# Score products of a differential attention head: from two packed 128-row products per map to three 64-row products on the two halves of the array

## The chip, the cores and the metric

The kernel runs on one core of one Trainium2 chip. The metric is the device time of one execution in microseconds (us), the median of several runs. The profile shown is one execution that the hardware profiler recorded.

## The reference, cut to what matters

One layer of a hybrid encoder block on 512 tokens plus 16 meta tokens (L = 528 keys), 1024 channels, float32. After an RMSNorm, one projection gives the operands of two attention branches of eight heads each: stick-breaking attention, and differential attention. Then come gates, an output projection and a SwiGLU feed-forward. The change is in the differential branch:

```
dq = df_q.reshape(B, L_pad, DF_HEADS, 2, DF_HEAD_DIM)   # two maps of 64 channels each per head
dk = df_k.reshape(B, L_pad, DF_HEADS, 2, DF_HEAD_DIM)
s = jnp.einsum('bhcqd,bhckd->bhcqk', q, k) * (DF_HEAD_DIM ** -0.5)
s = jnp.where(mask, s - slope * dist, -jnp.inf)
p = jax.nn.softmax(s, axis=-1)
w = p[:, :, 0] - lam * p[:, :, 1]
o = jnp.einsum('bhqk,bhkd->bhqd', w, v)
```

So each head has two score maps (c = 0 and 1), and each map is a product over 64 channels. The channels of both maps together are the 128 columns that one projection block of a head gives.

## The kernel before, in words

All float32 products are made of parts: an operand is split into a high part (rounded to the format fp32r) and a low part (the rest), and a product is the sum of high by high, high by low and low by high (`mm3`, lines 159 to 161, three instructions on TensorE that add up in the same PSUM bank). Each TensorE product is a weight load (LDWEIGHTS, 128 columns of the stationary operand) and a matmul that streams the moving operand.

The attention part is a loop over 16 heads, eight of the stick-breaking branch (`sb_head`) and then eight of the differential branch (`df_head`). While a head's attention runs, TensorE also makes the projections of the next head: `sb_units` and `df_units` give a list of units (two for q, two for k, two for v), `y_units` gives the branch's output projection of earlier heads, and the loop at line 748 puts units between the stages of a head wherever the head yields. So the TensorE work of a head's attention stands in several short groups between long runs of projection products. Outside the opening part of the kernel, which is ordered by hand, a scheduler places the instructions by priorities; evacuations of PSUM are issued with `tc.high_priority`.

Projection q and k of a stick-breaking head are kept as four tiles on 128 partitions: `qh`, `ql` (high and low part) and `kh`, `kl`. For a differential head the layout differs: for each map c one tile `dq` holds the 64 rows of that map's high part on the map's own half of the partitions and the low part on the other half, and one tile `dk` holds the high and the low part of k, both twice, once on each half of the partitions. So `q_evac` and `k_evac` of `df_units` work on 64 partitions at a time (lines 419, 420, 426, 427), and once per map a DMA on the GpSimd queue copies 64 rows to the other half (line 429).

With this layout the scores of one map over one block of keys need two products, each on all 128 rows:

```
nc.tensor.matmul(o, lhsT=q[c][:, qs], rhs=k[c][:, 0, k0:k1], start=True, stop=False)
nc.tensor.matmul(o, lhsT=q[c][:, qs], rhs=k[c][:, 1, k0:k1], start=False, stop=True)
```

The first gives high by high plus low by high, the second high by low plus low by low (lines 446 and 447).

A head has four query blocks t of 128 rows. `scores(0)`, `scores(1)` and `scores(2)` cover 256, 272 and 400 columns of keys for both maps; `scores3(c)` covers two halves of 264 columns for one map. Score tiles `z` are two PSUM banks each, and there are two of them. VectorE adds the position bias and takes the row maximum (`biased`, line 450), ScalarE takes the exponential (line 474), VectorE normalises and combines the two maps (lines 477 to 480), and TensorE transposes the result (line 315, and line 327 for small leftover blocks, which use 64 or 32 rows). Another partial product is the transposition of 33 rows of parameters at line 715.

Of the kernel before, what the change touches and what calls it, by code (L numbers as in the profile page):

```python
# [9 lines left out]
F32 = mybir.dt.float32  # L10
F32R = mybir.dt.float32r
# [5 lines left out]
P = 128  # L17
# [22 lines left out]
def block_kernel(ctx: ExitStack, tc: tile.TileContext, x, meta, norm_mix_g, w_in, w_gate, b_gate,  # L40
# [239 lines left out]
    def v_units(key, d):  # L280
        vT = ap_.tile([P, L], F32, tag="vT", bufs=1, name="vT")

        def turn():

            vf = ap_.tile([P, 2, P], F32, tag="vf", bufs=2, name="vf")
            vh = ap_.tile([P, 3, P], F32R, tag="vh", bufs=2, name="vh")
            vl = ap_.tile([P, 3, P], F32R, tag="vl", bufs=2, name="vl")
            pt, p5 = tr_tile(), tr_tile()
            for j in range(4):
                nc.tensor.transpose(pt[:, j * P:(j + 1) * P], vT[:, j * P:(j + 1) * P], ident)  # L290
            pv = pt.rearrange("p (j c) -> p j c", c=P)
            nc.scalar.copy(vh, pv[:, 0:3])
            nc.vector.tensor_tensor(vl, pv[:, 0:3], vh.bitcast(F32), op=ALU.subtract)
            nc.scalar.copy(vf[:, 0], pt[:, 3 * P:4 * P])
            for t in range(NQ):
                nc.gpsimd.tensor_copy(v_s[:, 32 * t:32 * t + NM], vT[:, (t + 1) * P:(t + 1) * P + NM])  # L296
            nc.tensor.transpose(p5[:, 0:P], v_s, ident)
            nc.scalar.copy(vf[:, 1], p5[:, 0:P])
            d["v"] = (vf, vh, vl)

        return kv_units(key, lambda ps, s: nc.scalar.copy(vT[:, s], ps)), turn  # L301
# [41 lines left out]
        return lambda: turn((0, 1)), turn_rest, weighted  # L343


    def sb_units(h):
        d = {}
        qh = ap_.tile([P, SEQ], F32R, tag="qh", bufs=2, name="qh")
        ql = ap_.tile([P, SEQ], F32R, tag="ql", bufs=2, name="ql")
        kh = ap_.tile([P, L], F32R, tag="kh", bufs=2, name="kh")  # L350
        kl = ap_.tile([P, L], F32R, tag="kl", bufs=2, name="kl")
        d["q"], d["k"] = (qh, ql), (kh, kl)

        def q_evac(ps):
            nc.scalar.activation(qh, ps, AF.Copy, scale=SB_SCALE)
            nc.vector.scalar_tensor_tensor(ql, ps, SB_SCALE, qh.bitcast(F32), op0=ALU.mult, op1=ALU.subtract)

        def k_evac(ps, s):
            nc.scalar.copy(kh[:, s], ps)
            nc.vector.tensor_tensor(kl[:, s], ps, kh[:, s].bitcast(F32), op=ALU.subtract)  # L360

        vu, turn = v_units(("sb", h, 2), d)
        return d, halves(("sb", h, 0), xT, QT, q_evac, h == 0) + kv_units(("sb", h, 1), k_evac) + vu, turn

    def sb_head(h, d, o_h, o_l):
        qh, ql = d["q"]
# [39 lines left out]
        nc.vector.tensor_tensor(o_l, ps, o_h.bitcast(F32), op=ALU.subtract)  # L406


    def df_units(h):
        d = {}  # L410
        hs = (slice(0, 64), slice(64, 128))
        q = [ap_.tile([P, SEQ], F32R, tag=("qh", "ql")[c], bufs=2, name=f"dq{c}") for c in range(2)]
        k = [ap_.tile([P, 2, L], F32R, tag=("kh", "kl")[c], bufs=2, name=f"dk{c}") for c in range(2)]
        d["q"], d["k"] = q, k

        def q_evac(ps):
            for c in range(2):
                a, b = hs[c], hs[1 - c]
                nc.scalar.activation(q[c][a], ps[a], AF.Copy, scale=DF_SCALE)
                nc.vector.scalar_tensor_tensor(q[c][b], ps[a], DF_SCALE, q[c][a].bitcast(F32),  # L420
                                               op0=ALU.mult, op1=ALU.subtract)

        def k_evac(ps, s):
            for c in range(2):
                a = hs[c]
                nc.scalar.copy(k[c][a, 0, s], ps[a])
                nc.vector.tensor_tensor(k[c][a, 1, s], ps[a], k[c][a, 0, s].bitcast(F32), op=ALU.subtract)  # L427
                if s.stop == L:
                    nc.gpsimd.dma_start(k[c][hs[1 - c]].bitcast(F32), k[c][a].bitcast(F32))

        vu, turn = v_units(("df", h, 2), d)
        return d, halves(("df", h, 0), xT, QT, q_evac) + kv_units(("df", h, 1), k_evac) + vu, turn

    late = []

    def df_head(h, d, o_h, o_l):
        q, k = d["q"], d["k"]
        bias = ap_.tile([P, L], F32, tag="bias", name="bias")
        nc.gpsimd.tensor_scalar(bias, dist, -(2.0 ** -(h + 1)), None, op0=ALU.mult)
        mx = small.tile([P, NQ, 2], F32, tag="mx", name="mx", bufs=2)  # L440
        ls = small.tile([P, NQ, 2], F32, tag="ls", name="ls", bufs=2)
        prs = [ap_.tile([P, 2, 144 + t * P], F32, tag=f"w{t}", name="pr") for t in range(NQ)]

        def score(o, t, c, k0, k1):
            qs = slice(t * P, (t + 1) * P)
            nc.tensor.matmul(o, lhsT=q[c][:, qs], rhs=k[c][:, 0, k0:k1], start=True, stop=False)  # L446
            nc.tensor.matmul(o, lhsT=q[c][:, qs], rhs=k[c][:, 1, k0:k1], start=False, stop=True)  # L447

        def biased(t, c, zz, po, bb):
            nc.vector.tensor_tensor_reduce(po, zz, bb, scale=1.0, scalar=-3.0e38, op0=ALU.add, op1=ALU.max,  # L450
                                           accum_out=mx[:, t, c:c + 1])

        def scores(t):
            n = 144 + t * P
            z = z_tile()
            for c in range(2):
                score(z[:, c, 0:max(n, 256)], t, c, 0, max(n, 256))
            for c in range(2):
                biased(t, c, z[:, c, 0:n], prs[t][:, c], bias[:, L - n:L])
            maps(t)  # L460

        def scores3(c):
            two = lambda v: v.rearrange("p (a b) -> p a b", a=2)
            z = z_tile()
            for hf in range(2):
                score(z[:, hf, 0:HL], 3, c, hf * HL, (hf + 1) * HL)
            biased(3, c, z[:, :, 0:HL], two(prs[3][:, c]), two(bias))

        def maps(t):
            pr = prs[t]  # L470
            nm = small.tile([P, 2], F32, tag="nm", name="nm")
            nc.vector.tensor_scalar(nm, mx[:, t], -1.0, None, op0=ALU.mult)  # L472
            for c in range(2):
                nc.scalar.activation(pr[:, c], pr[:, c], AF.Exp, bias=nm[:, c:c + 1], accum_out=ls[:, t, c:c + 1])  # L474
            with tc.high_priority(offset=EVAC):
                rc = small.tile([P, 2], F32, tag="rc", name="rc")
                nc.vector.reciprocal(rc, ls[:, t])
                nc.vector.tensor_tensor(rc[:, 1:2], rc[:, 1:2], nlam, op=ALU.mult)
                nc.vector.tensor_scalar(pr[:, 0], pr[:, 0], rc[:, 0:1], csc, op0=ALU.mult, op1=ALU.mult)
                nc.vector.scalar_tensor_tensor(pr[:, 0], pr[:, 1], rc[:, 1:2], pr[:, 0], op0=ALU.mult, op1=ALU.add)  # L480

        scores(0)
        scores(1)
        yield 1
        if late:
            late.pop(0)()
        scores(2)
        yield 1
        scores3(0)
        yield 1  # L490
        scores3(1)
        maps(3)
        t1, t2, av = attn_out(lambda t, k0, k1: prs[t][:, 0, k0:k1], d, 64)
        yield 3 if h < NH - 1 else 2
        t1()
        yield 1
        t2()
        yield 1
        ps = av()
        of = ap_.tile([P, SEQ], F32, tag="of", name="of")  # L500
        sq = ap_.tile([P, SEQ], F32, tag="sq", name="sq")
        sqh = ap_.tile([P, SEQ], F32R, tag="a_h", name="sqh")
        sql = ap_.tile([P, SEQ], F32R, tag="a_l", name="sql")
        nc.scalar.copy(of, ps)
        eng = nc.gpsimd if h < NH - 1 else nc.vector
        eng.tensor_tensor(sq, of, of, op=ALU.mult)
        split(sqh, sql, sq, lo_eng=eng)

        def norm():
            pv = tr_tile()  # L510
            nc.tensor.matmul(pv, lhsT=ones_r, rhs=sql, start=True, stop=False)
            nc.tensor.matmul(pv, lhsT=ones_r, rhs=sqh, start=False, stop=True)
            nc.scalar.activation(sq, pv, AF.Ln, bias=eps_c)
            nc.scalar.activation(sq, sq, AF.Exp, scale=-0.5)
            nc.vector.scalar_tensor_tensor(sq, pv, var_max, sq, op0=ALU.is_le, op1=ALU.mult)
            nc.vector.tensor_tensor(of, of, sq, op=ALU.mult)
            nc.scalar.activation(o_h, of, AF.Copy, scale=g_sub)
            nc.vector.scalar_tensor_tensor(o_l, of, g_sub, o_h.bitcast(F32), op0=ALU.mult, op1=ALU.subtract)  # L518

        late.append(norm)  # L520
# [594 lines left out]
```

## Time and profile before

| what | value |
|---|---|
| median of 3 runs | 992.69 us (992.54 to 994.67) |
| the profiled execution's own time | 992.9 us |
| its span, first to last instruction | 991.1 us |
| mean granted TensorE clock | 0.995 of full speed |
| busy time of TensorE matmuls (PE) | 970.6 us, 6285 instructions |
| busy time of weight loads (PEld) | 877.1 us |
| VectorE (DVE), ScalarE (ACT), GpSimd (POOL) | 662.0, 534.0, 110.0 us |

PE and PEld are two rows of the same engine: a weight load can run while the matmul before it streams. Matmuls are pipelined and the end of each is modelled, so a row's duration is longer than what the instruction costs in a stream; the time that one costs is read from the distance between the starts of neighbouring rows. L446 is line 446 of the kernel. A form such as 128x264 names partitions and elements per partition; in the form 33*128 of a matmul the first number is the rows of the stationary operand and the second its columns.

### The profile page before, as it was taken

The page shows a single profiled execution, that of the slowest core. Times are in us where ns is not written, and L with a number is a line of the kernel's source. Part 1 is how long each engine was busy: PE and PEld are TensorE (multiplying, and loading weights), DVE is VectorE, ACT ScalarE, POOL GpSimd, SP SyncE. Part 2 cuts the span into 40 slices and gives each one's busy share as a digit, 9 for nine tenths or more (in the row PEclk, how much of TensorE's full clock was granted, in tenths as well). Part 3 has the DMA queues.
Part 4 walks back from the last instruction along what each step waited for, and adds up shares of the span by engine and source line. Part 5 has one row for each costly group of instructions (what it writes and reads, how often), then busy time and mean ns, then how long its engine had stood idle before and what let it go on. Part 6 is the DMA issues. An engine that isn't in the chain of part 4 may idle for free.

```text
span 991.1 us, 16004 instructions
## 1 busy us (share of the span) xinstructions
PE 970.6 (98%) x6285; PEld 877.1 (88%) x6285; DVE 662.0 (67%) x1214; ACT 534.0 (54%) x1017; POOL 110.0 (11%) x152
## 2 busy tenths in 40 slices
PE   7999999999999999999999999989999999999996
PEld 5999899998899998899878888879999999988885
DVE  8665446666677876778763333798888888754644
ACT  5655554555455666556653333675555555743533
POOL 4000000000122211221112330000000000000103
PEclk9999999999999999999999999999999999999998
DMA  6322222221333323333223343233433333333212
GB/s 200 107 64 65 86 73 78 65 86 51 101 89 105 92 66 100 87 86 107 65 64 106 106 170 107 65 99 94 119 95 112 102 108 106 107 106 106 86 43 85
DMA packets 129742, 93.13 MB, mean 94 GB/s; under 512 B 3681, under 2 KB 114434, under 8 KB 129666
## 3 DMA queue, kind: packets, MB, share of 16 engines
q1 hardware_dynamic: 127506, 85.09, 28.3%
q0 software_dynamic: 2000, 6.95, 2.6%
q8 instruction: 49, 0.80, 0.3%
q14 instruction: 27, 0.22, 0.1%
q10 hardware_dynamic: 160, 0.07, 0.0%
HBM read 85.67 MB, written 2.10 MB: 89 GB/s over the span
## 4 chain that ended last, share of the span: by engine, by line
PE 90%; DVE 4%; ACT 3%; DMA 1%; issue 1%; POOL 0%; SPq 0%; DVEq 0%; ACTq 0%; POOLq 0%
PE mm L159 22%; PE mm L160 21%; PE mm L161 21%; PE z L159 6%; PE z L160 6%; PE z L161 6%; PE tr L315 2%; PE z L446 1%; PE z L447 1%; ACT wh L74 1%; PE tr L290 1%; PE z L339 0%; PE tr L327 0%; ACT bf L865 0%; DMA xs<-in_x_dram 0%
## 5 line engine op out<-in xcount | busy, mean ns | idle before, releaser
L75 DVE TENSOR_TENSOR wl<-wst,wh 128x1024 fp32r<-128x1024 f32 (+1 forms) x150 | 174.2, 1162 | 146.5 <-ACT wh L74 146.1
L159 PE MATMUL mm<-xT_h,wh 128*128 128x264 f32 (+2 forms) x776 | 249.9, 322 | 1.0 <-DVE dk L427 0.8
L160 PE MATMUL mm<-xT_l,wh 128*128 128x264 f32 (+2 forms) x776 | 247.3, 319 | 1.6 <-DVE xT_l L633 1.6
L161 PE MATMUL mm<-xT_h,wl 128*128 128x264 f32 (+2 forms) x776 | 246.8, 318 | 0.0
L74 ACT CAST wh<-wst 128x1024 fp32r<-128x1024 f32 (+1 forms) x150 | 148.6, 991 | 170.6 <-PE mm L160 113.2
L159 PEld LDWEIGHTS mm<-xT_h,wh 128*128 128x128 f32 x776 | 146.8, 189 | 11.3 <-PE tr L315 1.0
L160 PEld LDWEIGHTS mm<-xT_l,wh 128*128 128x128 f32 x776 | 146.8, 189 | 10.9 <-DVE xT_l L633 1.8
L161 PEld LDWEIGHTS mm<-xT_h,wl 128*128 128x128 f32 x776 | 146.7, 189 | 9.9
L160 PE MATMUL mm<-hT_l,wh 128*128 128x256 f32 x284 | 80.5, 284 | 0.7 <-DVE hT_l L862 0.7
L159 PE MATMUL mm<-hT_h,wh 128*128 128x256 f32 x284 | 80.1, 284 | 0.5 <-DVE sg L993 0.5
L161 PE MATMUL mm<-hT_h,wl 128*128 128x256 f32 x284 | 80.1, 283 | 0.0
L160 PEld LDWEIGHTS mm<-hT_l,wh 128*128 128x128 f32 x284 | 53.7, 189 | 1.2 <-DVE hT_l L862 1.1
L159 PEld LDWEIGHTS mm<-hT_h,wh 128*128 128x128 f32 x284 | 53.4, 189 | 0.9 <-DVE sg L993 0.8
L161 PEld LDWEIGHTS mm<-hT_h,wl 128*128 128x128 f32 x284 | 53.6, 189 | 0.0
L159 PE MATMUL mm<-o_h,wh 128*128 128x512 f32 x128 | 53.2, 415 | 0.0
L160 PE MATMUL mm<-o_l,wh 128*128 128x512 f32 x128 | 50.0, 391 | 0.8 <-DVE o_l L518 0.8
L161 PE MATMUL mm<-o_h,wl 128*128 128x512 f32 x128 | 50.1, 391 | 0.0
L159 PE MATMUL mm<-t_h,wh 128*128 128x256 f32 x168 | 47.4, 282 | 1.3 <-ACT wh L74 1.0
L160 PE MATMUL mm<-t_l,wh 128*128 128x256 f32 x168 | 47.3, 281 | 1.1 <-DVE t_l L877 1.1
L161 PE MATMUL mm<-t_h,wl 128*128 128x256 f32 x168 | 47.3, 281 | 0.0
L296 POOL COPY v_s<-vT 128x16 f32<-128x16 f32 x64 | 21.8, 370 | 210.0 <-ACT vT L301 210.0
L474 ACT ACTIVATE pr<-pr,nm 128x144 f32<-128x144 f32 (+3 forms) x64 | 36.3, 569 | 14.2 <-DVE nm L472 14.1
(275 smaller groups left out, 2226.5 us busy)
## 6 DMA issues: line engine op xcount, KB each, us to landing
wst<-in_w_in_dram SPq DMA_DIRECT2D x46, 512.0 KB, 3.9
wst<-in_w_ffn_gate_dram SPq DMA_DIRECT2D x22, 512.0 KB, 3.9
wst<-in_w_ffn_down_dram SPq DMA_DIRECT2D x22, 512.0 KB, 3.5
wsu<-in_w_ffn_up_dram SPq DMA_DIRECT2D x21, 512.0 KB, 3.7
wst<-in_w_gate_dram SPq DMA_DIRECT2D x16, 512.0 KB, 4.0
dk<-dk POOLq DMA_DIRECT2D x16, 264.0 KB, 5.1
wst<-in_w_br_sb_dram SPq DMA_DIRECT2D x8, 512.0 KB, 3.5
wst<-in_w_br_df_dram SPq DMA_DIRECT2D x8, 512.0 KB, 3.6
```

Source lines behind the costliest of these rows:

```text
L74: (hi_copy or nc.scalar.copy)(hi, src)
L75: (lo_eng or nc.vector).tensor_tensor(lo, src, hi.bitcast(F32), op=ALU.subtract)
L159: nc.tensor.matmul(ps, lhsT=ah, rhs=bh, start=(start and i == 0), stop=False, skip_group_check=skip)
L160: nc.tensor.matmul(ps, lhsT=ah, rhs=bl, start=False, stop=False, skip_group_check=skip)
L161: nc.tensor.matmul(ps, lhsT=al, rhs=bh, start=False, stop=(stop and i == n - 1), skip_group_check=skip)
L290: nc.tensor.transpose(pt[:, j * P:(j + 1) * P], vT[:, j * P:(j + 1) * P], ident)
L296: nc.gpsimd.tensor_copy(v_s[:, 32 * t:32 * t + NM], vT[:, (t + 1) * P:(t + 1) * P + NM])
L315: nc.tensor.transpose(pt[:, (t - j) * P:(t - j + 1) * P], blocks(t, j * P, (j + 1) * P), ident)
L446: nc.tensor.matmul(o, lhsT=q[c][:, qs], rhs=k[c][:, 0, k0:k1], start=True, stop=False)
L447: nc.tensor.matmul(o, lhsT=q[c][:, qs], rhs=k[c][:, 1, k0:k1], start=False, stop=True)
L474: nc.scalar.activation(pr[:, c], pr[:, c], AF.Exp, bias=nm[:, c:c + 1], accum_out=ls[:, t, c:c + 1])
```

## The change: what it does, and the diff

`df_units` becomes the same function as `sb_units`, called with the other branch's name and scale: q and k of a differential head stay on 128 partitions as `qh`, `ql`, `kh`, `kl`, with map 0 on partitions 0 to 63 and map 1 on partitions 64 to 127. The four half-width evacuations of q and the eight of k per head become two and four of full width, and the two DMAs per head go. `score` now makes, for one block of keys, three products for each of the two maps, each on 64 rows only (`q[r, qs]`, `k[r, k0:k1]`), and the two maps take turns: map 0, map 1, map 0 and so on, on the two halves of the array's rows and into different PSUM banks. `scores3` makes both maps at one place, after both yields, and so takes both `z` tiles at once; before, one map stood in front of the second yield and one behind it.

```
-    def sb_units(h):
+    def qkv_units(br, h):
         d = {}
+        scale = (SB_SCALE, DF_SCALE)[br == "df"]
         qh = ap_.tile([P, SEQ], F32R, tag="qh", bufs=2, name="qh")
         ql = ap_.tile([P, SEQ], F32R, tag="ql", bufs=2, name="ql")
         kh = ap_.tile([P, L], F32R, tag="kh", bufs=2, name="kh")
...
         def q_evac(ps):
-            nc.scalar.activation(qh, ps, AF.Copy, scale=SB_SCALE)
-            nc.vector.scalar_tensor_tensor(ql, ps, SB_SCALE, qh.bitcast(F32), op0=ALU.mult, op1=ALU.subtract)
+            nc.scalar.activation(qh, ps, AF.Copy, scale=scale)
+            nc.vector.scalar_tensor_tensor(ql, ps, scale, qh.bitcast(F32), op0=ALU.mult, op1=ALU.subtract)
 
         def k_evac(ps, s):
             nc.scalar.copy(kh[:, s], ps)
             nc.vector.tensor_tensor(kl[:, s], ps, kh[:, s].bitcast(F32), op=ALU.subtract)
 
-        vu, turn = v_units(("sb", h, 2), d)
-        return d, halves(("sb", h, 0), xT, QT, q_evac, h == 0) + kv_units(("sb", h, 1), k_evac) + vu, turn
+        vu, turn = v_units((br, h, 2), d)
+        return d, halves((br, h, 0), xT, QT, q_evac, (br, h) == ("sb", 0)) + kv_units((br, h, 1), k_evac) + vu, turn
+
+    def sb_units(h):
+        return qkv_units("sb", h)
+
+    def df_units(h):
+        return qkv_units("df", h)
...
-    def df_units(h):
-        d = {}
-        hs = (slice(0, 64), slice(64, 128))
-        q = [ap_.tile([P, SEQ], F32R, tag=("qh", "ql")[c], bufs=2, name=f"dq{c}") for c in range(2)]
-        k = [ap_.tile([P, 2, L], F32R, tag=("kh", "kl")[c], bufs=2, name=f"dk{c}") for c in range(2)]
-        d["q"], d["k"] = q, k
-
-        def q_evac(ps):
-            for c in range(2):
-                a, b = hs[c], hs[1 - c]
-                nc.scalar.activation(q[c][a], ps[a], AF.Copy, scale=DF_SCALE)
-                nc.vector.scalar_tensor_tensor(q[c][b], ps[a], DF_SCALE, q[c][a].bitcast(F32),
-                                               op0=ALU.mult, op1=ALU.subtract)
-
-        def k_evac(ps, s):
-            for c in range(2):
-                a = hs[c]
-                nc.scalar.copy(k[c][a, 0, s], ps[a])
-                nc.vector.tensor_tensor(k[c][a, 1, s], ps[a], k[c][a, 0, s].bitcast(F32), op=ALU.subtract)
-                if s.stop == L:
-                    nc.gpsimd.dma_start(k[c][hs[1 - c]].bitcast(F32), k[c][a].bitcast(F32))
-
-        vu, turn = v_units(("df", h, 2), d)
-        return d, halves(("df", h, 0), xT, QT, q_evac) + kv_units(("df", h, 1), k_evac) + vu, turn
-
...
     def df_head(h, d, o_h, o_l):
-        q, k = d["q"], d["k"]
+        (qh, ql), (kh, kl) = d["q"], d["k"]
...
-        def score(o, t, c, k0, k1):
+        def score(os, t, k0, k1):
+
             qs = slice(t * P, (t + 1) * P)
-            nc.tensor.matmul(o, lhsT=q[c][:, qs], rhs=k[c][:, 0, k0:k1], start=True, stop=False)
-            nc.tensor.matmul(o, lhsT=q[c][:, qs], rhs=k[c][:, 1, k0:k1], start=False, stop=True)
+            for i, (q, k) in enumerate(((qh, kh), (qh, kl), (ql, kh))):
+                for c in range(2):
+                    r = slice(64 * c, 64 * c + 64)
+                    nc.tensor.matmul(os[c], lhsT=q[r, qs], rhs=k[r, k0:k1], start=(i == 0), stop=(i == 2))
...
         def scores(t):
             n = 144 + t * P
             z = z_tile()
-            for c in range(2):
-                score(z[:, c, 0:max(n, 256)], t, c, 0, max(n, 256))
+            m = max(n, 256)
+            score([z[:, c, 0:m] for c in range(2)], t, 0, m)
             for c in range(2):
                 biased(t, c, z[:, c, 0:n], prs[t][:, c], bias[:, L - n:L])
             maps(t)
 
-        def scores3(c):
+        def scores3():
             two = lambda v: v.rearrange("p (a b) -> p a b", a=2)
-            z = z_tile()
+            z = [z_tile() for _ in range(2)]
             for hf in range(2):
-                score(z[:, hf, 0:HL], 3, c, hf * HL, (hf + 1) * HL)
-            biased(3, c, z[:, :, 0:HL], two(prs[3][:, c]), two(bias))
+                score([z[c][:, hf, 0:HL] for c in range(2)], 3, hf * HL, (hf + 1) * HL)
+            for c in range(2):
+                biased(3, c, z[c][:, :, 0:HL], two(prs[3][:, c]), two(bias))
...
         scores(2)
         yield 1
-        scores3(0)
         yield 1
-        scores3(1)
+        scores3()
         maps(3)
```

## Rows read from the trace of the kernel before

**Rows 1.** The page: busy time by engine, and the chain by engine.

```profile
PE 970.6 (98%) x6285; PEld 877.1 (88%) x6285; DVE 662.0 (67%) x1214; ACT 534.0 (54%) x1017; POOL 110.0 (11%) x152
...
PE 90%; DVE 4%; ACT 3%; DMA 1%; issue 1%; POOL 0%; SPq 0%; DVEq 0%; ACTq 0%; POOLq 0%
```

**Rows 2.** Busy time by stretch; from:to, length, engines in order, clock, DMA, GB/s.

```profile
274.00:497.00 223.00, 223.00 (x1439) 201.94 (x1438) 169.17 (x423) 136.82 (x316) 47.39 (x64) 1.00 0.31 89
```

**Rows 3.** Timeline of TensorE, scores of the last head; start and duration in us.

```profile
472.97 0.28 PE L446 MATMUL z<-dk,dq 128*128 128x256 f32 x1
...
473.44 0.29 PE L446 MATMUL z<-dk,dq 128*128 128x272 f32 x1
...
473.94 0.39 PE L159 MATMUL mm<-o_h,wh 128*128 128x512 f32 x1
...
477.14 0.34 PE L446 MATMUL z<-dk,dq 128*128 128x400 f32 x1
...
477.86 0.39 PE L159 MATMUL mm<-o_h,wh 128*128 128x512 f32 x1
...
480.60 0.28 PE L446 MATMUL z<-dk,dq 128*128 128x264 f32 x1
...
481.10 0.40 PE L159 MATMUL mm<-xT_h,wh 128*128 128x512 f32 x1
```

**Rows 4.** Line 446: its matmuls and their forms; line 447 has the same.

```profile
L446 PE MATMUL z<-dk,dq x80: 278/286/347, 262.7 to 484.1; 128*128 128x264 f32 x32, 128*128 128x256 f32 x16, 128*128 128x272 f32 x16, 128*128 128x400 f32 x16
```

**Rows 5.** Timeline of the weight loads, two in a row after transposes.

```profile
490.23 0.19 PEld L159 LDWEIGHTS mm<-xT_h,wh 128*128 128x128 f32 x1
490.33 0.19 PEld L160 LDWEIGHTS mm<-xT_l,wh 128*128 128x128 f32 x1
```

**Rows 6.** Timeline around line 715, a product of 33 rows among full ones.

```profile
33.23 0.28 PE L160 MATMUL mm<-xT_l,wh 128*128 128x264 f32 x1
...
33.35 0.28 PE L161 MATMUL mm<-xT_h,wl 128*128 128x264 f32 x1
...
33.56 0.13 PEld L715 LDWEIGHTS mm<-ident,prow 33*128 33x128 f32 x1
...
33.74 0.39 PE L159 MATMUL mm<-xT_h,wh 128*128 128x264 f32 x1
33.85 0.19 PEld L160 LDWEIGHTS mm<-xT_l,wh 128*128 128x128 f32 x1
33.97 0.28 PE L160 MATMUL mm<-xT_l,wh 128*128 128x264 f32 x1
```

**Rows 7.** Evacuations of q and k: ScalarE's and VectorE's groups, shapes kept apart; busy us, mean ns.

```profile
L426 ACT CAST dk<-mm 64x264 fp32r<-64x264 f32 x32 | 12.0, 374 | 14.0 <-DVE dk L427 12.7 <-PE mm L161 0.4
L419 ACT ACTIVATE dq<-mm 64x512 fp32r<-64x512 f32 x16 | 9.4, 589 | 0.9 <-DVE dq L420 0.8
...
L427 DVE TENSOR_TENSOR dk<-mm,dk 64x264 fp32r<-64x264 f32 x32 | 13.7, 429 | 2.5 <-ACT dk L426 1.7
...
L420 DVE SCALAR_TENSOR_TENSOR dq<-mm,dq 64x512 fp32r<-64x512 f32 x16 | 11.0, 688 | 0.5
```

**Rows 8.** Timeline of TensorE where the first differential head is projected; waits in brackets.

```profile
245.80 0.60 PE L315 MATMUL tr<-ident,s 128*128 128x128 f32 x4
246.56 0.52 PE L315 MATMUL tr<-ident,s 128*128 128x128 f32 x3 [0.15 <-DVE dq L420]
247.89 0.36 PE L159 MATMUL mm<-xT_h,wh 128*128 128x264 f32 x1 [0.81 <-DVE dk L427]
```

**Rows 9.** Line 450 by form; then timelines of VectorE and ScalarE, last head.

```profile
L450 DVE CUSTOM_DVE_ANT_0 pr<-z,bias 128x528 f32<-128x528 f32 x16 | 11.3, 705 | 2.0 <-PE z L447 1.8
...
486.54 0.16 DVE L472 TENSOR_SCALAR nm<-mx 128x2 f32<-128x2 f32 x1
...
487.03 1.05 ACT L74 CAST wh<-wst 128x1024 fp32r<-128x1024 f32 x1 [2.55 <-PE mm L160]
488.56 0.73 ACT L474 ACTIVATE pr<-pr,nm 128x528 f32<-128x528 f32 x1
```

## The prediction

> **What bounds the kernel now.** I read the page's busy times and its chain first: TensorE is busy for 970.6 of 991.1 us and holds 90% of the chain that ended last, while VectorE has a third of the span free and ScalarE nearly half [rows 1]. Then I cut the span into stretches, because a share of the whole says nothing of the place that is changed. From 274 us, in the first differential head, to 497 us, just behind the last, TensorE is busy for 223.00 of 223.00 us at full clock [rows 2]. So in this stretch every nanosecond that TensorE's instruction stream gains or loses is a nanosecond of the kernel, and work taken off the other engines is worth nothing unless TensorE waits for it. The reader should see that busy here doesn't mean that TensorE couldn't be faster: a row's 0.28 us is a latency, and the cost is the step from start to start. So next I read the timeline of the scores of one head.
>
> **What the scores cost now.** The eight products of `scores(0)` and `scores(1)` run from 472.97 to 473.94: four of 256 columns take 0.47 us, four of 272 take 0.50. Four of 400 columns run from 477.14 to 477.86, 0.72 us. Four of 264 run from 480.60 to 481.10, 0.50 us, and there are two such groups [rows 3]. That is 0.47 + 0.50 + 0.72 + 2 x 0.50 = 2.69 us a head, and the counts (80 on each of the two lines, 10 a head) say that the eight heads are alike [rows 4]: 21.5 us in all. This is all that the change can shorten on TensorE, and at these steps (0.12, 0.125, 0.18 and 0.125 us) a product costs its columns.
>
> **The products, part by part.** Four products of 128 rows (two maps, two products) become six of 64 rows (two maps, three products). There are five such sets in a head. No row of this trace shows two products on different halves of the rows, so I bound it. If each pair runs side by side at today's step, a set costs three steps in place of four: a quarter of 2.69 us, 0.67 us a head, 5.4 us gained. If nothing overlaps, it costs six steps, 1.5 x 2.69 us: 10.8 us lost. I take the side-by-side end: the two products of a pair read different partitions, use different rows of the array and write different banks, and neither needs the other's result. I keep the other end as a rival.
>
> The Trainium skill ("TensorEngine Tiling (Array Packing)", Key Properties) says that different tiles execute weight loads and matmuls in parallel, and its table gives up to twice the speed for a short dimension of at most 64. No run here shows that yet; the sum by it is the 5.4 us gained, before what follows.
>
> **The change of shape.** Now the group of 64-row products stands among 128-row products, and the trace has one place that shows what that costs: the transpose of 33 rows at line 715 [rows 6]. Steps of 264 columns are 0.12 us there. After the full matmul at 33.35 the weight load of the 33-row product starts only at 33.56, after 0.21 us: 0.09 us beyond the step. In a run of full products the load of the next weights lies under the matmul before; here it begins only when that one has left. On the way back, the first full product starts at 33.74 and the next at 33.97, 0.23 us in place of 0.12: its own weight load, 0.11 us, is bare. Two loads in a row start 0.11 us apart (33.74 and 33.85) there, and 0.10 us apart elsewhere [rows 5, 6], so a load of 128 columns takes about 0.105 us of the load path. From 33.56 to 33.74 lie the 33-row product's own work and the emptying behind it, so the emptying on the way back is between 0 and 0.18 us; I take 0.09, as on the way in.
>
> So a round trip costs 0.09 + 0.105 (in: emptying, and the bare first load) + 0.09 + 0.105 (out: the same) = 0.39 us. Where is each? The scores of a head stand in three groups: blocks 0 and 1 together, block 2, and block 3, whose two maps now stand in one place. Three groups in eight heads are 24 round trips, 9.4 us. That is more than the 5.4 us that the products can give.
>
> The Trainium skill speaks against the change at this point: the same page, under Key Properties, says that changing the tiling mode, not just the tile, drains TensorE. It gives no figure; the trace agrees with the rule by its 0.09 us, and the sum goes by that row.
>
> **Evacuations, DMAs and waits.** Per head ScalarE's two casts of q at 589 ns and four of k at 374 become one and two at nearly the same length, as the elements per partition stay; VectorE's likewise, 688 and 429 ns [rows 7]. That frees 1.34 us of ScalarE and 1.55 us of VectorE a head, and on GpSimd the issue of two DMAs, behind which the small copies of v stand in its queue; the transfers themselves load no instruction of TensorE, whose stretch is full. All this is worth nothing where TensorE doesn't wait, which is everywhere from 274 us on. The exception lies before it: while the first differential head is projected, TensorE waits for these evacuations. Four transposes from 245.80 reach 246.56 and three more 247.89, 2.09 us for seven that cost about 0.11 us each, so some 1.3 us is lost there [rows 8]. With half the evacuation work I take 1.0 us as given back; the bounds are 0 and 1.3.
>
> `scores3` puts the sum with the bias of map 0 behind both maps, so one more instruction of 0.705 us stands on VectorE between the last score product and the exponential. In heads 0 to 6 it takes the place of evacuations (1.55 us less) in the same queue. In the last head, which projects nothing, the scaled maximum is ready at 486.54 + 0.16 us, but ScalarE takes up the exponential only at 488.56, behind a weight cast that began at 487.03 and what follows it [rows 9]; a delay of 0.705 us disappears in that gap. I put it at 0; without that cover it would be up to 0.7 us. `scores3` also takes both score tiles at once; the last reader of the one is two projection units back as before, so no new wait stands there, and if one did, it would hold up projection units queued behind it on TensorE.
>
> **The sum** is made against the profiled execution, 992.9 us (its span of 991.1 and 1.8 around it), which lies 0.2 above the median of 992.69: 992.9 - 5.4 + 9.4 - 1.0 = 995.9 us. Slower by 0.3%.
>
> **Rivals.** A: as above, 995.9. Its own range is 993 to 999, from the emptying on the way out (0 to 0.18 us, 24 times, 2.2 us either way) and the wait at 246 us.
>
> B, the loads queue: products overlap, but the two halves share one path for weight loads. Then a set of six loads costs 6 x 0.105 = 0.63 us, more than three steps of any width here (0.35 to 0.54), and the loads set the pace: five sets cost 3.15 us a head. A has 2.02 us of steps and three bare first loads, 0.315, in that place; B adds the last product of each group behind its last load (0.125 + 0.18 + 0.125 = 0.43). So B is 3.15 + 0.43 - 2.33 = 1.25 us a head above A: 1005.9. For it: in full products the loads follow one another on one path with 0.10 us each [rows 5]. Against it: those loads use all rows, and here each uses half. It decides as soon as two loads need over 0.18 us.
>
> C, no overlap at all: six steps for three, 2.02 us a head above A: 1012.0. For it: all matmul starts in this trace come one after the other. Against it: none of them could have overlapped.
>
> D, the other side, faster: the halves overlap and the switch is free, because the 0.39 us at line 715 belongs to that small transpose and not to the row count. Then 992.9 - 5.4 - 1.0 = 986.5. It decides if a round trip costs less than 0.22 us (5.4 / 24). For it: line 715 differs in data type and width too. Against it: the load behind it is bare by a full 0.11 us, which width and type of the product before don't explain.
>
> E, half a switch: the emptying remains, the bare loads are hidden by loading the free half early: 24 x 0.18 = 4.3 us, and 992.9 + 4.3 - 5.4 - 1.0 = 990.8, at the edge of no change.
>
> **How the numbers follow.** About 0.2%, 2 us, can be told from no change. Chances: A 0.45, B 0.25, C 0.10, D 0.12, E 0.08. Slower by more than 0.2%: B, C and most of A (0.37, the part above 994.9), 0.72. Faster: D and half of E, 0.16. Same: the rest, 0.12. The time is A's against the median, 995.9 - 0.2, rounded up for a switch inside a group that the scheduler may add (0.39 us): 996.0. The range of 987 to 1010 leaves out C and half of D (0.16) and holds B with its uncertainty.
>
> **What would show it.** After the change: six rows a set with forms of 64 rows; the starts of a pair a few hundredths of a microsecond apart and the pairs 0.12 to 0.18 apart (A), or loads evenly 0.1 us apart (B), or matmuls a full step apart (C). Before each group's first load a step longer than the last full product's by 0.09, and the second full product behind a group late by 0.11; neither of them, and it is D. Three groups a head: more, and the scheduler has cut them. The waits near 246 us should be nearly gone. I am wrong if the switch is cheaper than 0.22 us a round trip, or if halves don't overlap.

## The result, and the profile after

The changed kernel takes 996.54 us (median of 10 runs) where the kernel before takes 993.14 on the same chips: a ratio of 1.0032, 95% interval 1.0023 to 1.0041. It is slower by 3.4 us; 3.3 were forecast (996.0 against 992.69).

The page of the changed kernel, busy times, against the first line of [rows 1]:

```profile
PE 975.4 (98%) x6365; PEld 871.9 (88%) x6365; DVE 645.9 (65%) x1190; ACT 521.6 (52%) x993; POOL 103.2 (10%) x136
```

All three other engines lost work (VectorE 16 us, ScalarE 12, GpSimd 7) and the kernel became longer; only the busy time of TensorE's matmuls grew. That alone says where to look. The timeline of TensorE at blocks 0 and 1 of the last head of the changed kernel, against [rows 3] (start, duration; x2 are two products in one row):

```profile
474.68 0.39 PE L160 MATMUL mm<-o_l,wh 128*128 128x512 f32 x1
474.91 0.39 PE L161 MATMUL mm<-o_h,wl 128*128 128x512 f32 x1
475.23 0.39 PE L432 MATMUL z<-kh,qh 64*128 64x256 f32 x2
475.46 0.28 PE L432 MATMUL z<-kl,qh 64*128 64x256 f32 x2
475.58 0.28 PE L432 MATMUL z<-kh,ql 64*128 64x256 f32 x2
475.69 0.29 PE L432 MATMUL z<-kh,qh 64*128 64x272 f32 x2
475.82 0.29 PE L432 MATMUL z<-kl,qh 64*128 64x272 f32 x2
475.94 0.29 PE L432 MATMUL z<-kh,ql 64*128 64x272 f32 x2
476.16 0.51 PE L159 MATMUL mm<-o_h,wh 128*128 128x512 f32 x1
476.50 0.40 PE L160 MATMUL mm<-o_l,wh 128*128 128x512 f32 x1
```

The weight loads of the same stretch:

```profile
474.69 0.19 PEld L161 LDWEIGHTS mm<-o_h,wl 128*128 128x128 f32 x1
475.23 0.19 PEld L432 LDWEIGHTS z<-kh,qh 64*128 64x128 f32 x2 [0.35 <-issue]
475.33 0.19 PEld L432 LDWEIGHTS z<-kl,qh 64*128 64x128 f32 x2
475.46 0.19 PEld L432 LDWEIGHTS z<-kh,ql 64*128 64x128 f32 x2
```

Three things are to be seen. First, two products share a step: 475.46 to 475.58 and on in steps of 0.11 to 0.13 us, as one product of that width needed before, and two loads start in each step as well. Second, the way in: from 474.91 to 475.23 is 0.32 us where the step of 512 columns is 0.23, and the first load starts only then, not under the product before; the first pair's own step is 0.23 in place of 0.12. Third, the way out: 475.94 to 476.16 is 0.22 for 0.125, and 476.16 to 476.50 is 0.34 for 0.23. So a visit costs 0.09 + 0.11 + 0.09 + 0.11 = 0.40 us. The whole group, from first pair to the next full product, takes 0.93 us against 0.97 [rows 3], and the 0.04 gained there are paid back five times by 0.20 at its two edges (0.09 in front, 0.11 behind). The trace has 24 such groups, as forecast, with the same excess at the edges of each. Over six whole heads, from 291.46 to 475.23 (first score products of the second and of the last head), the changed kernel takes 183.77 us, where the kernel before takes 180.57 (292.40 to 472.97): 0.53 us a head, 4.3 in eight, for products and switches together.

Where the first differential head is projected, the waits of [rows 8] are gone:

```profile
245.81 0.93 PE L315 MATMUL tr<-ident,s 128*128 128x128 f32 x7
246.50 0.37 PE L159 MATMUL mm<-xT_h,wh 128*128 128x264 f32 x1
```

Seven transposes take 0.69 us, where they took 2.09: 1.40 us given back.

The evacuations by group, shapes kept apart, against [rows 7]:

```profile
L360 ACT CAST kh<-mm 128x264 fp32r<-128x264 f32 x32 | 11.7, 364 | 0.9 <-PE mm L161 0.9
L356 ACT ACTIVATE qh<-mm 128x512 fp32r<-128x512 f32 x16 | 9.5, 591 | 1.2 <-PE mm L161 1.2
...
L361 DVE TENSOR_TENSOR kl<-mm,kh 128x264 fp32r<-128x264 f32 x32 | 13.7, 428 | 0.4 <-ACT kh L360 0.2
L357 DVE SCALAR_TENSOR_TENSOR ql<-mm,qh 128x512 fp32r<-128x512 f32 x16 | 10.9, 683 | 1.2 <-ACT qh L356 1.2
```

The counts are the same as before, but now they serve sixteen heads in place of eight: twice the partitions at the same time each.

The last head in ScalarE's timeline, against [rows 9] (in brackets the idle time ahead, and what ended it):

```profile
489.53 0.74 ACT L460 ACTIVATE pr<-pr,nm 128x528 f32<-128x528 f32 x1 [3.47 <-DVE nm L458]
...
491.56 1.05 ACT L74 CAST wh<-wst 128x1024 fp32r<-128x1024 f32 x1
```

and in TensorE's:

```profile
493.38 0.55 PE L315 MATMUL tr<-ident,pr 128*128 128x128 f32 x3 [0.26 <-DVE pr L466]
```

The exponential of block 3 now waits for the maximum (3.47 us idle in front of it), and the weight cast that stood ahead of it before stands behind it: the gap in which the later maximum was to disappear isn't there. TensorE's matmuls wait 0.26 us for what comes out of that chain.

### The profile page after: what moved, and what is told of

Same layout as the page of the kernel before. It is cut to its first block, busy times and chain, and to the rows that moved or that the text cites. A ratio compares the mean times of both kernels' runs of the same rounds, so it can differ in the third digit from the quotient of the medians.

```text
span 995.3 us, 16034 instructions
## 1 busy us (share of the span) xinstructions
PE 975.4 (98%) x6365; PEld 871.9 (88%) x6365; DVE 645.9 (65%) x1190; ACT 521.6 (52%) x993; POOL 103.2 (10%) x136
## 4 chain that ended last, share of the span: by engine, by line
PE 90%; DVE 5%; ACT 3%; DMA 1%; issue 0%; POOL 0%; SPq 0%; DVEq 0%; ACTq 0%; POOLq 0%
PE mm L159 22%; PE mm L160 21%; PE mm L161 21%; PE z L159 6%; PE z L160 6%; PE z L161 6%; PE z L432 2%; PE tr L315 2%; ACT wh L74 1%; PE tr L290 1%; PE z L339 0%; PE tr L327 0%; ACT bf L850 0%; DMA xs<-in_x_dram 0%; DMA wsu<-in_w_ffn_up_dram 0%
## 5 line engine op out<-in xcount | busy, mean ns | idle before, releaser
L296 POOL COPY v_s<-vT 128x16 f32<-128x16 f32 x64 | 24.0, 403 | 259.8 <-ACT vT L301 259.8
```

## The experiments

**Half products on one half.** Is the gain in the products the overlap of the two halves?

```
-                    r = slice(64 * c, 64 * c + 64)
+                    r = slice(0, 64)
```

> The changed kernel with both maps' products on rows 0 to 63, so that map 1 is computed from map 0's channels; as many products of the same size in the same order, the array switched as often. Theory (the gain is the two halves working side by side): six steps a set in place of three, 2.02 us a head more, 1012.7 us. Rival (a product of 64 rows costs less by itself): 996.5 us.

Measured: 1012.14 us, 1.0185 of the kernel before (1.0168 to 1.0202). The timeline of its first group shows a pair in each row and twice the distance between rows:

```profile
262.03 0.40 PE L432 MATMUL z<-kl,qh 64*128 64x256 f32 x2
262.27 0.39 PE L432 MATMUL z<-kh,ql 64*128 64x256 f32 x2
262.50 0.41 PE L432 MATMUL z<-kh,qh 64*128 64x272 f32 x2
```

A pair on one half takes 0.23 to 0.24 us, two steps. A product of 64 rows is no cheaper than one of 128; sharing a step with the other half is worth 15.6 us here (forecast 16.2).

**The same six products on all rows.** What does the switch cost, with the number of products and their steps held?

```
-                    r = slice(64 * c, 64 * c + 64)
+                    r = slice(0, P)
```

> The changed kernel with the six products of a set on all 128 rows, so that both maps get the sum over all channels; the switch of the array's shape goes and so does the overlap. Theory (24 round trips of 0.39 us): beside the kernel with all products on one half, which should give 1012.7 us, it is 9.4 us faster: 1003.3 us, 10.2 us above the kernel before, as six steps a set for four and the lighter evacuations (-1.4) and the later last head (+0.5) give. Rival (what stands around the groups is no switch): 1012.7 us.

Measured: 1002.94 us, 1.0094 of before (1.0079 to 1.0109). Against the run on one half it is 9.2 us less, or 0.38 us for each of 24 round trips. Its group ends without the edge: the last pair of its first group and the next two full products, in its timeline, start 0.25 and 0.24 us apart,

```profile
262.39 0.41 PE L432 MATMUL z<-kh,ql 128*128 128x272 f32 x2
262.64 0.40 PE L159 MATMUL mm<-xT_h,wh 128*128 128x512 f32 x1
262.88 0.39 PE L160 MATMUL mm<-xT_l,wh 128*128 128x512 f32 x1
```

which is two steps of 272 columns, and one of 512.

**The evacuations alone.** What is the new layout worth where TensorE does as much score work as before?

```
-            for i, (q, k) in enumerate(((qh, kh), (qh, kl), (ql, kh))):
-                for c in range(2):
-                    r = slice(64 * c, 64 * c + 64)
-                    nc.tensor.matmul(os[c], lhsT=q[r, qs], rhs=k[r, k0:k1], start=(i == 0), stop=(i == 2))
+            for c in range(2):
+                for i, (q, k) in enumerate(((qh, kl), (ql, kh))):
+                    nc.tensor.matmul(os[c], lhsT=q[:, qs], rhs=k[:, k0:k1], start=(i == 0), stop=(i == 1))
```

> The changed kernel with two products of 128 rows per map (high by low and low by high over all channels; high by high is left out and the maps are not kept apart): TensorE's score work is that of the kernel before, and only the layout, its evacuations, the missing DMAs and the place of the last block's scores differ from it. Theory: 993.1 - 1.4 (wait at the first differential head) + 0.5 (last head) = 992.2 us. Rival (evacuations and DMAs are worth nothing, or cost): 993.1 us or more.

Measured: 992.28 us, 0.9989 of before (0.9979 to 0.9998): 1.1 us faster, as the theory has it, though the interval (0.2 to 2.1 us) nearly reaches no change and can't tell 0.9 from 1.4. Half the evacuation work, 16 DMAs less, and about a thousandth of the time. The second term of the theory is not in this run. In its last head the sums of both maps stand behind both products too, but cast and exponential keep the order of the kernel before,

```profile
486.19 1.05 ACT L74 CAST wh<-wst 128x1024 fp32r<-128x1024 f32 x1 [2.54 <-PE mm L160]
...
487.72 0.73 ACT L459 ACTIVATE pr<-pr,nm 128x528 f32<-128x528 f32 x1
```

and the maximum, ready at 486.42, is in time for it: the 0.5 us of the last head isn't lost here.

**One map after the other.** Does the turn-taking make the overlap?

```
-            for i, (q, k) in enumerate(((qh, kh), (qh, kl), (ql, kh))):
-                for c in range(2):
+            for c in range(2):
+                for i, (q, k) in enumerate(((qh, kh), (qh, kl), (ql, kh))):
```

> The changed kernel with one edit: the three products of map 0 stand ahead of the three of map 1, in place of taking turns. Theory (only neighbours on different halves overlap): in a group of two sets three of twelve products still meet a neighbour on the other half, so 9 steps where 6 were, and 5 for 3 in the group of one set; at 0.122 and 0.18 us a step that is 3 x 0.122 + 2 x 0.18 + 3 x 0.122 = 1.09 us a head, 8.7 us in all: 1005.3 us. Rival (the engine pairs products by itself, or half-size products are simply cheap): as the changed kernel, 996.5 us.

Measured: 996.3 us, 1.0032 of before (1.0021 to 1.0043), the changed kernel's own ratio. The theory fell. The timeline has the pairs of the changed kernel:

```profile
262.15 0.39 PE L432 MATMUL z<-kh,qh 64*128 64x256 f32 x2
262.38 0.29 PE L432 MATMUL z<-kl,qh 64*128 64x256 f32 x2
262.50 0.29 PE L432 MATMUL z<-kh,ql 64*128 64x256 f32 x2
```

That the scheduler kept the text's order, three and three, stands in no view directly, but the trace's own start times speak for it: in each of the 24 groups the first two products start 10 ns apart (262.151 and 262.161 here), where turns give 3 or 4 ns (475.228 and 475.232 in the changed kernel), as if two more products had been issued between them. So the fourth product of that order starts with the first.

**Six and then six.** How far ahead does a half find its work? Block 3 is made map by map over both its sets:

```
+            for one in range(2):
             for hf in range(2):
-                score([z[c][:, hf, 0:HL] for c in range(2)], 3, hf * HL, (hf + 1) * HL)
+                    score([z[c][:, hf, 0:HL] if c == one else None for c in range(2)], 3, hf * HL, (hf + 1) * HL)
```

> The changed kernel with the maps one after the other over the whole of block 3: six products on rows 0 to 63, then six on rows 64 to 127 (three and three in the other blocks). After the run with three and three, which was as fast as turns and whose halves started together, theory: each half takes its products from the queue on its own, at least six products ahead, so the time stays 996.5 us and the first product of the second half starts within some 0.02 us of the first. Rival (the halves can only look a few products ahead): part of the last six runs alone, up to 6 steps of 0.122 us in each of eight heads, up to 5.9 us more, 1002 us.

Measured: 999.18 us, 1.0057 of before (1.0041 to 1.0072). Neither number: 2.9 us above the run with three and three (2.5 by the two ratios to the kernel before). The timeline of block 3 in the first head:

```profile
272.06 0.39 PE L433 MATMUL z<-kh,qh 64*128 64x264 f32 x1
272.29 0.28 PE L433 MATMUL z<-kl,qh 64*128 64x264 f32 x1
272.42 0.28 PE L433 MATMUL z<-kh,ql 64*128 64x264 f32 x1
272.42 0.39 PE L433 MATMUL z<-kh,qh 64*128 64x264 f32 x2
272.65 0.28 PE L433 MATMUL z<-kl,qh 64*128 64x264 f32 x2
272.77 0.28 PE L433 MATMUL z<-kh,ql 64*128 64x264 f32 x2
272.89 0.28 PE L433 MATMUL z<-kh,qh 64*128 64x264 f32 x1
273.02 0.28 PE L433 MATMUL z<-kl,qh 64*128 64x264 f32 x1
273.14 0.28 PE L433 MATMUL z<-kh,ql 64*128 64x264 f32 x1
```

The second half starts when the third of the first half's six has started, so three products run alone at each end and three overlap. Three steps of 0.12 us in eight heads are 2.9 us, the whole difference, and all eight heads show it. The score tile of the second half had been read out on VectorE at 268.26, so a wait for it isn't the reason. So the halves do draw from the queue on their own, but only a few products ahead: if the queue holds the order of the text, which no view shows, a product four behind the newest one started did overlap, and one five behind did not.

**Four groups a head.** Does a round trip cost the same when only their number is changed?

```
         scores(0)
+        yield 1
         scores(1)
         yield 1
...
         scores(2)
         yield 1
-        yield 1
         scores3()
```

> The changed kernel with one projection unit moved between block 0 and block 1 (it stood between blocks 2 and 3 together with another): the same instructions, but four groups of 64-row products a head in place of three. Theory (a round trip costs 0.39 us wherever it is): 8 more, 3.1 us: 999.7 us. Rival (the cost is in the number of products, not of groups): 996.5 us.

Measured: 1007.46 us, 1.0143 of before (1.013 to 1.0157), 10.9 us more in place of 3.1. The edit did more than it was meant to. The timeline of block 3 in the second head:

```profile
304.44 0.28 PE L432 MATMUL z<-kl,qh 64*128 64x264 f32 x1
304.56 0.28 PE L432 MATMUL z<-kh,ql 64*128 64x264 f32 x1
304.76 0.39 PE L159 MATMUL mm<-xT_h,wh 128*128 128x264 f32 x1
305.08 0.38 PE L432 MATMUL z<-kh,qh 64*128 64x264 f32 x1
```

The scheduler took block 3's maps apart in seven of eight heads and put one full product between them, two in the last head (one unit later than block 2 only one of the two score tiles can have been free; that reason is argued, not shown). That gives 39 groups for 24, and six unpaired steps more in seven heads: 15 x 0.39 + 7 x 6 x 0.122 = 11.0 us, against 10.9 measured. As a test of the theory it is worth less than it looks, since both terms were found afterwards, but one full product between two halves shows what a misplaced instruction costs: a switch and the overlap.

**Two groups a head.** And with fewer?

```
         scores(0)
         scores(1)
+        scores(2)
         yield 1
         if late:
             late.pop(0)()
-        scores(2)
         yield 1
         yield 1
         scores3()
...
-            z = z_tile()
             m = max(n, 256)
-            score([z[:, c, 0:m] for c in range(2)], t, 0, m)
+            if t:
+                z2 = z_tile()
+                z = [z2[:, c] for c in range(2)]
+            else:
+                z = [mm_tile() for _ in range(2)]
+            score([z[c][:, 0:m] for c in range(2)], t, 0, m)
```

> The changed kernel with blocks 0, 1 and 2 in one group (block 0's two score tiles taken from the banks of the projections): two groups of 64-row products a head in place of three. Theory: 8 fewer round trips, 3.1 us less: 993.4 us, level with the kernel before. Rival (a bank or VectorE holds up the longer group): above 995 us, with waits of TensorE on VectorE in front of block 2 or of a projection unit.

Measured: 992.93 us, 0.9997 of before (0.9988 to 1.0006): 3.6 us below the changed kernel, level with the kernel before. Of the 3.6, eight round trips at 0.39 are 3.1; the rest lies within the interval, and the last head's wait for VectorE's result is also missing from its list of waits.

**Two groups, and block 3 of the last head earlier.**

```
-        yield 1
+        if h < NH - 1:
+            yield 1
         scores3()
         maps(3)
+        if h == NH - 1:
+            yield 1
```

> The kernel with two groups a head, and block 3 of the last head one projection unit earlier, so that its exponentials are not late. Theory (the changed kernel lost 0.5 us at the last head's transposes because the sum with the bias of both maps stands behind both): 992.9 - 0.5 = 992.4 us, 0.1% below the kernel before, at the edge of what can be told. Rival (a score tile isn't free so early, and the scheduler takes the maps apart): 993 to 994 us.

Measured: 992.66 us, 0.9991 of before (0.9982 to 1.0000). It beats the changed kernel clearly and the kernel before by less than can be told. Whether the last head gives anything on top of two groups stays open: the two ratios to the kernel before differ by 0.0006, 0.6 us, and each has an interval of 0.9 us to either side.

**The other partial products made full**, in the kernel before.

```
-                b = blocks(t, (t + 1) * P - 32 * t, (t + 1) * P + NM)
-                nc.tensor.transpose(pt[0:32 * t + NM, t * qn:(t + 1) * qn], b[lo_rows:P], ident[lo_rows:P, lo_rows:P])
+                k0 = (t + 1) * P - 32 * t
+                b = wide(t, k0, k0 + P) if wide else blocks(t, k0, (t + 1) * P + NM)
+                nc.tensor.transpose(pt[0:b.shape[1], t * P:(t + 1) * P], b, ident)
```

> The kernel before, with its only other partial products made full: the four small leftover transposes of every head (32 rows in the stick-breaking branch, 64 in the differential one) read all 128 rows; in the differential branch they also have all 128 columns, in the other their 16 to 112. Theory (each group of partial products costs a round trip of 0.39 us): 16 round trips less, 6.2 us; four full transposes cost 0.109 us each for 0.056 (differential) and some 0.033 (the other), 1.7 and 2.4 us more: 2.1 us faster, 991.0 us. Rival (few columns switch the array as well): the stick-breaking half then keeps its switch and pays 2.4 us: 994 us.

Measured: 994.17 us, 1.0011 of before (1.0002 to 1.002): slower by 0.8 where 2.1 were to be gained. The number is the rival's, but its reason isn't. The timeline of the leftover transposes in a stick-breaking head, of this kernel:

```profile
79.48 0.49 PE L315 MATMUL tr<-ident,s 128*128 128x128 f32 x3
79.80 0.60 PE L328 MATMUL tr<-ident,s 128*16 128x128 f32 x4
80.16 0.39 PE L159 MATMUL mm<-xT_h,wh 128*128 128x264 f32 x1
80.39 0.28 PE L160 MATMUL mm<-xT_l,wh 128*128 128x264 f32 x1
```

and of the kernel before:

```profile
79.38 0.49 PE L315 MATMUL tr<-ident,s 128*128 128x128 f32 x3
79.80 0.31 PE L327 MATMUL tr<-ident,s 32*16 32x32 f32 x4
80.06 0.39 PE L159 MATMUL mm<-xT_h,wh 128*128 128x264 f32 x1
80.29 0.28 PE L160 MATMUL mm<-xT_l,wh 128*128 128x264 f32 x1
```

With few columns and all rows nothing is lost on the way in: three full transposes take 0.32 us up to the first small one, and the four small ones 0.36. In the kernel before, three transposes and the way in take 0.42 us, 0.09 more. So it is the rows that switch the array. From the first full transpose to the second full product behind, both kernels take 0.91 us: four transposes on all rows cost as much as the round trip that they save. By their starts the transposes of 32 rows take 0.033 us each, so that round trip is about 4 x (0.109 - 0.033) = 0.30 us, an estimate, and 0.1 less than my 0.39. Its first load has 16 columns and a record of 0.08 us, where one of 128 columns has 0.19; that this makes the difference is argued, not shown.

That explains why nothing is gained in the stick-breaking half, not why 0.8 is lost. The loss stands in the differential half: from the leftover transposes of the first head to those of the seventh, this kernel takes 181.10 us (286.93 to 468.03), the kernel before 180.58 (286.70 to 467.28), 0.09 us a head more, 0.7 in eight. In five of these seven heads the weight load in front of them waits for VectorE in both kernels; in the first head of this kernel

```profile
286.93 0.42 PEld L328 LDWEIGHTS tr<-ident,pr 128*128 128x128 f32 x4 [0.28 <-DVE y_sb L536]
```

and of the kernel before:

```profile
286.70 0.25 PEld L327 LDWEIGHTS tr<-ident,pr 64*16 64x16 f32 x4 [0.32 <-DVE y_sb L534]
```

There an emptying that is saved may lie under the wait, while the transposes behind it are longer, 0.109 for 0.056 us each. But two heads have no such wait (346.63 and 376.70 in the kernel before) and lose as much, so the cause of the 0.8 stays open.

**Both edits on the changed kernel.**

> The changed kernel with both edits: two groups of 64-row products a head, and the leftover transposes on all rows. Theory: 996.5 - 3.1 - 2.1 = 991.3 us, below both kernels. Rival as for the two edits by themselves: 994 us or more.

Measured: 993.38 us, 0.9999 of before (0.999 to 1.0008), neither the theory's number nor the rival's. As the single edits: two groups bring it level, full transposes add nothing.

## Why the prediction was right, step by step

**What bounds the stage** held: the work that went from VectorE, ScalarE and GpSimd brought 1.1 us, and the steps that TensorE gained or lost arrived in the total.

**The products** (forecast 5.4 us gained): pairs share steps as taken. Products and switches together cost 4.3 us by the whole heads, against 9.4 - 5.4 = 4.0. With the 9.2 of the switches the products gave 4.9; with 24 x 0.40 = 9.6 from the rows, 5.3. Rival C is out by the shared steps and by the run on one half. Rival B, loads that queue, is out by the weight-load rows above: two loads start in each step, 0.12 us, where one path would need 0.21. A load of one half is no shorter than a full one: in the run with six and six the first product, alone on its half, takes 0.23 us to the next (272.06 to 272.29), a step of 0.12 and a bare load of 0.11. (B would have shown at 256 columns as soon as two loads need over 0.12 us, not only over 0.18.)

**The switch** (forecast 0.39 us a round trip, 9.4 in all): 0.40 by the rows, 9.2 by the two runs whose edits differ in nothing but the rows. The 0.09 on the way out was a guess between bounds of 0 and 0.18, and it was right. Rival D falls with it, and E too: the first load starts only 0.09 us after the step of the full product before it. The prediction was wrong that line 715 is the one place of the trace before that shows the price: the leftover transposes of line 327 show it in the stick-breaking heads, with the same 0.09 us on the way in and about 0.30 for the round trip. At that price, by estimate, 24 round trips would have been 7.2 us in place of 9.4.

**The evacuations** (forecast 1.0 us): 1.40 by the rows, just above the upper bound of 1.3, since I had counted 0.11 us for each of seven transposes and they took 0.10. The run with the evacuations alone, 1.1 with an interval of 0.2 to 2.1, agrees with either.

**The last head** was forecast at 0, and that was wrong for the changed kernel: a later maximum was to disappear in the gap in front of the exponential. In the run with the evacuations alone it does. In the changed kernel the scheduler put the weight cast behind the exponential, and TensorE waits 0.26 us at the transposes. Between the last two normalisations (line 496, 479.03 to 503.23) it takes 24.20 us, before 23.53 (476.68 to 500.21), and 23.56 with the evacuations alone. Two groups stand in this stretch and cost (0.75 + 0.20 - 0.72) + (0.93 + 0.20 - 1.00) = 0.36 us, so 0.3 is left for the last head. Its bound of 0.7 held. How the 0.3 comes about is not isolated: the run with six products on all rows has the changed kernel's order (exponential at 495.79, cast at 497.81), and its list of waits doesn't have this one.

So the sum of what was measured, 4.3 - 1.4 + 0.3 = 3.2 us, agrees with the 3.4 of the medians (interval 2.3 to 4.1). That the forecast of 3.3 comes so near is in part luck: 0.4 more was given back and 0.3 more went to products and switches, and the 0.3 of rounding, put there for a switch inside a group that doesn't occur (the trace has exactly 24 groups), is as large as the loss in the last head that had been put at 0. The range of 987 to 1010 would have held rival B too; what tells A from the others is the rows.

## What to carry to other kernels

Count groups before you count products: a visit to half-row products costs about 0.4 us here, for an emptying and a bare weight load at either end, with three pairs in it as with six, so it pays only if it saves more than that, and the first thing to change is the number of visits, not the work in them. Read the price off any odd-shaped product that the kernel already has (here one transpose of 33 rows), but compare other such places, for the price may depend on that product's own size: behind the small transposes it is about 0.3. A gap that hides a delay belongs to the schedule that made it; when instructions can be placed anew, look for what would still stand there.

## What the runs showed that I had not expected

The two halves don't need turns. With three products of one half ahead of three of the other the halves start together (262.15, both in one row) and the time is the same; with six ahead of six, three overlap. The Trainium skill ("TensorE: Matmul & The Clock Gate", Part 3) says that matmuls keep the program's order strictly in their starts and ends; by the text's order these two runs differ: with three and three, the second half's first product starts in the step of the first half's first although two others stand between.

Few columns don't switch the array: transposes with 16 to 112 columns of weights on all rows follow full ones without the 0.09 us (79.48 to 79.80 in the kernel with full transposes).

The profiled execution of the changed kernel is 4.2 us longer in span than that of the kernel before, more than the medians say. Some of it is elsewhere: by stretch, columns as in [rows 2],

```profile
662.00:664.00 2.00, 1.87 (x8) 1.87 (x9) 2.00 (x3) 1.29 (x3) 0.59 (x1) 0.50 0.88 260
```

the granted clock is 0.50, the lower of the two levels, behind a stretch in which TensorE stood still for 0.97 us waiting for a weight cast. In the profiled execution of the kernel before TensorE stands still as long for the same cast (0.97 us, up to 659.13), and the clock behind it is 1.00, so the wait alone doesn't lower it; what does stays open. Products of 256 columns take 0.21 us there in place of 0.12, for a little more than one microsecond in all. It doesn't follow the change: the kernel before with the full transposes shows a clock of 0.50 there too (660 to 662 us), and the changed one with two groups doesn't.
